# A decoder block on one core: 32 of the 640 dense expert tokens gathered instead, with their buffers, pacing and one inverse root moved

## The chip, the cores and the metric

The kernel runs on one core of a Trainium2 chip. The metric is the device time of one execution in microseconds (us); lower is better. Every time and row below belongs to an execution on the chip.

## The reference

One decoder layer on 1024 tokens of width 1024, in float32:

```python
x = x + concat(gated_deltanet(h), sliding_window_attention(h)) @ w_out
x = x + peer(rmsnorm(x))
x = x + sigmoid(rmsnorm(x) @ w_g) * (p @ w_p)
out = rmsnorm(x)
```

What matters here is `peer`, retrieval of single-neuron experts. For each token and each of 8 heads, two queries are scored against 128 keys each; the best 16 of each half are combined, and of the 256 sums the best 16 name experts out of 128 x 128 = 16384. So each token has 128 experts (8 heads x 16), each with a gate from a softmax over its head:

```python
act = gelu(einsum("td,thkd->thk", x, u_tab[expert]))
y   = einsum("thk,thkd->td", gates * act, v_tab[expert])
```

`u_tab` and `v_tab` have 16384 rows of 1024 float32 each (64 MB a table).

## The kernel before

Tokens are worked in eight blocks of 128. There are three large stages.

**Upstream** (`upstream`, L327). Projections, DeltaNet and attention (`mixing`), then retrieval (`retrieving`, L383) in four groups of two blocks. For a group, `retrieve` (L398) multiplies by the output weights, takes the norm, stores its transposed halves (`h2Td`, L435 and L436, for the dense blocks) or the tokens themselves (`h2d`, L431, for the gathered ones), makes the queries, and takes the top 16 of each half (`first_topk`, L749) and of the combinations (`topk`, L757). `topk` turns positions back into indices with comparisons and sums over 16-wide axes, on a tile of KC = 16 results at a time (L786 to L808). Weights are loaded on SP's queue, four pairs deep.

**Two ways through the experts.** Blocks 0 to 4 (`DBLK`) go the dense way: for them every expert is computed, and a table G of gates, mostly zero, selects. `gbuild` (L837) makes that table for one block in eight slices of 16 tokens (`TB`): for four tokens at a time it compares an iota with the two indices (one VectorE instruction, L845), scales by the gate (four on ScalarE, L847), multiplies (four on TensorE) and copies out; a slice is written to DRAM (`gd`, L853). Blocks 5 to 7 (`ABLK`) go the gathered way: for each of a token's 128 experts one indirect DMA fetches 128 rows of 4 KB, one per token and partition.

**Dense stage** (`dense`, L924). A loop over 128 chunks of 128 experts, in 32 groups of four (`GC`). A chunk loads its 512 KB of each table, splits them into a high and a low part (`split`, L167: ScalarE copies, VectorE subtracts), and multiplies with the 640 dense tokens in two parts of 320 columns, three products (`mm3`, L141) for each of eight slices of the width: 48 matmuls. ScalarE takes the gelu, VectorE multiplies by the group's part of G (`Gt`, loaded at L969), and the product is split again (`wh`, `wl`). After four chunks, each token block is multiplied with the second table in two halves of 512 columns, 30 matmuls a chunk; the tokens are the stationary operand there. Blocks 0 and 1 stay in PSUM to the end (`HELD`), the others are added to `xB` on VectorE (L1009).

**Gathering beside it.** `gather_job` (L904) is a generator that yields after each gather. For a block, `gather_dots` (L862) loads the tokens (`h2n`), fetches 128 times from `u` with a dot product on VectorE each (L868), and takes gelu times gate; `gather_block` (L875) fetches 128 times from `v` with a multiply-add each (L882) into `acc`, which starts as the residual and is stored back. `h2n` and `acc` share one buffer (tag `hacc`). Fetches are issued by POOL (`fetched`, L856). Their tiles alternate between two pools, `gp` with four and `gx` with three buffers, opened after upstream (L1069, L1070), where retrieval's tiles lie before.

What sets the order: the program is scheduled when it is built, by a simulated clock and the order in which it is written, and each engine then runs its own instructions in that fixed order. `step` (L946) hands out gathers evenly over 448 steps (128 chunks and 32 x 10 half blocks):

```python
n = total * count[0] // steps - count[1]
count[1] += n
advance(n)
```

`held_back` (L895) forbids that the VectorE instruction of a gather be placed before the step that lies two (`LAG`) back. DMAs other than gathers go through SP's queue in order.

**Final stage** (`final`, L1013). The last gate for blocks 5, 6, 0, 1, 2, 3, 4, 7 in this order. `pre` (L1033) takes a norm: square with a sum on ScalarE, inverse root on POOL (`rsqrt`, L154: a multiply-add and a power), scaling on VectorE, eight transposes and a split. `gate_weights` (L1020) loads and splits eight 512 KB slices; `post` (L1047) has 48 matmuls of 512 columns a block.

## Time and profile before

| | |
|---|---|
| median of 3 runs | 3034.56 us (3032.35 to 3036.15) |
| the profiled execution | 3043.6 us |
| its span, first to last instruction | 3041.8 us |
| mean granted TensorE clock | 0.986 of 2.4 GHz |
| HBM | 766.40 MB read, 99.61 MB written |
| gathers | 768 (384 from `u`, 384 from `v`) |

In all views PE is TensorE's matmul, PEld its weight load, DVE VectorE, ACT ScalarE, POOL GpSimd and SP SyncE, whose rows are DMA issues. Times are us from the span's start unless marked ns. Busy time of PE is modelled and pipelined: a row's duration is longer than the distance to the next start, so the rate of matmuls is read from starts. A row of groups has the operation, its tiles (out<-in), shapes and count, then busy us and mean ns of one, then the idle time just before them on that engine and what ended most of it. "L79", "L82", "L76" and "L136" are helpers that many places use, so tiles name the operation.

### The profile page before, as it was taken

The numbers are of one execution on the slowest core, as the hardware profiler recorded it, in microseconds if no ns is written. First come the engines' busy times: TensorE is split into PE (matmuls) and PEld (weight loads), VectorE is DVE, ScalarE is ACT, GpSimd is POOL, SyncE is SP. The second block draws the span as 40 slices with busy tenths as digits, with TensorE's granted clock in tenths as the row PEclk, the third lists the DMA queues.
The fourth block names the chain that finished last, engine by engine and source line by source line (L and its number), as shares of the span: only waits on it lengthen the run. The fifth ranks groups of instructions, "written<-read, shape, count | busy, mean of one in ns | idle before, by whom it ended". The sixth has DMA issues, their size and how long they took to land. (4 is left out here: it accounts for less than half of the span.)

```text
span 3041.8 us, 49726 instructions
## 1 busy us (share of the span) xinstructions
PE 2936.2 (97%) x18287; PEld 2690.0 (88%) x18287; DVE 2499.4 (82%) x5023; ACT 1234.6 (41%) x2761; POOL 1068.4 (35%) x901
## 2 busy tenths in 40 slices
PE   7999999999999889999999999999999999999988
PEld 5887999999998789999999989998898898998967
DVE  5658636898999779988699889887998898899974
ACT  5556634488777663222222222232232232222223
POOL 0000000000000000765356556554656565556541
PEclk9989999999999999999999999999999999999989
DMA  7569657689889994999799989888999899899962
GB/s 236 142 223 364 206 191 248 215 223 243 237 242 270 287 279 141 351 338 348 272 342 354 330 319 369 329 332 300 335 351 345 318 358 332 306 337 347 324 256 89
DMA packets 449955, 869.30 MB, mean 286 GB/s; under 512 B 193456, under 2 KB 235824, under 8 KB 445360
## 3 DMA queue, kind: packets, MB, share of 16 engines
q1 hardware_dynamic: 339120, 463.43, 46.5%
q0 software_dynamic: 110592, 402.70, 36.4%
q8 instruction: 143, 2.34, 0.3%
q14 instruction: 100, 0.82, 0.1%
HBM read 766.40 MB, written 99.61 MB: 285 GB/s over the span
## 5 line engine op out<-in xcount | busy, mean ns | idle before, releaser
L136 PE MATMUL bk_u<-hT,uh 128*128 128x320 f32 x4096 | 915.4, 310 | 7.0 <-DMA hT<-h2Td 3.7
L136 PEld LDWEIGHTS bk_u<-hT,uh 128*128 128x128 f32 x4096 | 695.7, 189 | 23.2 <-ACT ge L988 4.6
L858 POOL DMA_INDIRECT rows<-in_u_dram,eidx x384 | 499.1, 1300 | 555.5 <-DVE dots L868 283.1
L136 PE MATMUL bk_u<-hT,ul 128*128 128x320 f32 x2048 | 635.0, 310 | 0.3 <-DVE ul L79 0.3
L858 POOL DMA_INDIRECT rows<-in_v_dram,eidx x384 | 498.6, 1298 | 350.1 <-DVE acc L82 287.5
L82 DVE SCALAR_TENSOR_TENSOR acc<-rows,dots,acc 128x1024 f32<-128x1024 f32 x384 | 492.2, 1282 | 35.4 <-DMA rows<-in_v_dram,eidx 24.5
L868 DVE CUSTOM_DVE_ANT_0 rows<-rows,h2n 128x1024 f32<-128x1024 f32 x384 | 459.9, 1223 | 27.5 <-DMA rows<-in_u_dram,eidx 27.3
L136 PEld LDWEIGHTS bk_u<-hT,ul 128*128 128x128 f32 x2048 | 386.5, 189 | 4.1 <-DVE ul L79 0.7
L988 ACT ACTIVATE ge<-bk_u 128x320 f32<-128x320 f32 x256 | 109.8, 431 | 603.3 <-PE bk_u L136 552.6
L136 PE MATMUL bk_y<-vh,wh 128*128 128x512 f32 x768 | 298.9, 391 | 3.0 <-DVE xB L79 3.0
L136 PE MATMUL bk_y<-vl,wh 128*128 128x512 f32 x768 | 299.9, 392 | 0.0
L136 PE MATMUL bk_y<-vh,wl 128*128 128x512 f32 x768 | 296.8, 393 | 2.6 <-DVE wl L79 2.6
L76 ACT ACTIVATE wh<-ge 128x320 fp32r<-128x320 f32 x256 | 118.7, 469 | 316.7 <-DVE ge L79 304.1
L76 ACT ACTIVATE o<-o,tT 128x128 f32<-128x128 f32 x640 | 204.5, 392 | 56.4 <-DVE o L79 55.1
L76 ACT ACTIVATE uh<-ur 128x1024 fp32r<-128x1024 f32 x128 | 135.3, 1057 | 226.4 <-PE bk_u L136 217.5
L136 PE MATMUL bk_gm<-o 128*128 128x128 f32 x1280 | 203.2, 286 | 22.5 <-ACT o L76 16.2
L136 PE MATMUL bk_s<-h,whi 128*128 128x256 f32 x1024 | 209.1, 295 | 3.3 <-DMA whi<-wqc 1.0
L79 DVE TENSOR_TENSOR o<-iota,tT 128x1024 f32<-128x1024 f32 x160 | 194.7, 1220 | 11.5 <-PE bk_gm L136 8.9
L136 PEld LDWEIGHTS bk_gm<-o 128*128 128x128 f32 x1280 | 178.2, 195 | 29.0 <-ACT o L76 20.2
L136 PE MATMUL bk_yp<-vl,wh 128*128 128x512 f32 x512 | 199.7, 391 | 0.0
L136 PE MATMUL bk_yp<-vh,wh 128*128 128x512 f32 x512 | 199.1, 391 | 0.0
L79 DVE TENSOR_TENSOR xB<-bk_y,xB 128x512 f32<-128x512 f32 x192 | 131.1, 689 | 79.5 <-PE bk_y L136 79.1
(302 smaller groups left out, 5840.5 us busy)
## 6 DMA issues: line engine op xcount, KB each, us to landing
ur<-in_uT_dram SPq DMA_DIRECT2D x128, 512.0 KB, 6.8
vr<-in_v_dram SPq DMA_DIRECT2D x128, 512.0 KB, 6.7
gd<-stage SPq DMA_DIRECT2D x40, 1024.0 KB, 7.3
Gt<-gd SPq DMA_DIRECT2D x32, 1280.0 KB, 9.6
wlo<-wqc SPq DMA_DIRECT2D x128, 256.0 KB, 4.6
whi<-wqc SPq DMA_DIRECT2D x128, 256.0 KB, 4.7
whi<-woc SPq DMA_DIRECT2D x64, 256.0 KB, 4.8
wlo<-woc SPq DMA_DIRECT2D x64, 256.0 KB, 4.7
```

The source lines that it names most:

```text
L76: return S.activation(o, i, AF.Copy, **k)
L79: return V.tensor_tensor(o, a, b, op)
L82: return V.scalar_tensor_tensor(o, a, s, b, op0, op1, **k)
L136: PE.matmul(o, l, r, start=start, stop=stop)
L858: G.indirect_dma_start(out=r, out_offset=None, in_=tab, in_offset=bass.IndirectOffsetOnAxis(ap=eidx[:, u, s:s + 1], axis=0))
L868: held_back(V.tensor_tensor_reduce(out=r, in0=r, in1=h2n, op0=ALU.mult, op1=ALU.add, scale=1.0, scalar=0.0, accum_out=dots[:, s:s + 1]))
L988: S.activation(ge, pa, AF.Gelu_apprx_tanh)
```

## The change

- The last 32 tokens of block 4 leave the dense way. `NU` and `NT` become 608, the parts 304 columns; `gbuild` makes six slices for block 4, and `h2Td`, the second product and the sum into `xB` take 96 tokens of it.
- For these 32 tokens a new `gather_part` runs ahead of block 5. Four slots share a row of partitions: partition 32 g + t holds slots 32 g to 32 g + 31 of token t, so that 32 gathers of 128 rows from each table do for 32 x 128 experts. The indices and gates get into that layout through DRAM (`peidx`, `pegate`), the tokens are stored once (`ph2d`) and loaded four times, and a matmul with a 0/1 matrix (`fold`) adds the four partial sums into the rows of `xB`.
- The pool `gp` is opened before retrieval and has three buffers, `gx` four. To make room, `topk` works on KC = 8 results at a time.
- 832 gathers are handed out over 31/32 of the 448 steps, that is by step 434.
- The first inverse root of the final stage is taken by Newton steps on VectorE.

```diff
+CUT = 32
+NU = len(DBLK) * 128 - CUT
-GBUF = 4
-GXBUF = 3
+GBUF = 3
+GXBUF = 4
+    fold = cp.tile([P, P], F32, name="fold")
+        nc.sync.dma_start(fold, I["fold"])
     def rsqrt(pool, dst, src, scale, n):
+        if newton[0]:
+            v, i, t = (pool.tile([P, n], d, tag=f"rn{m}{n}", name="rn_" + m)
+                       for m, d in (("v", F32), ("i", I32), ("t", F32)))
+            V.tensor_scalar(v, src, scale, EPS, op0=ALU.mult, op1=ALU.add)
+            V.tensor_scalar(i, v.bitcast(I32), 1, None, op0=ALU.logical_shift_right)
+            V.tensor_scalar(i, i, -1.0, 1597463007.0, op0=ALU.mult, op1=ALU.add)
+            y = i.bitcast(F32)
+            for it in range(3):
+                tt(t, y, y, ALU.mult)
+                stt(t, t, -0.5, v, ALU.mult, ALU.mult)
+                stt(dst if it == 2 else y, t, 1.5, y, ALU.add, ALU.mult)
+            return
+            pools["gp"] = ctx.enter_context(tc.tile_pool(name="gp", bufs=GBUF, side="right", reuse_waits="tile"))
             with ExitStack() as es:
                 lt = es.enter_context(tc.tile_pool(name="lt", bufs=1, side="right", reuse_waits="tile"))
+                if b == LB:
+                    nc.sync.dma_start(ph2d, h[LP:P, :])
-        KC = 16
+        KC = 8
+        if b == LB:
+            pe = tk.tile([P, P], I32, tag="pe", name="pe")
+            stt(pe, i1, 128.0, i2, ALU.mult, ALU.add)
+            nc.sync.dma_start(peidx, pe[LP:P, :])
+            nc.sync.dma_start(pegate, ga[LP:P, :])
+            for g in range(P // CUT):
+                nc.sync.dma_start(pidx[g * CUT:(g + 1) * CUT, :], peidx[:, g * CUT:(g + 1) * CUT])
+                nc.sync.dma_start(pgate[g * CUT:(g + 1) * CUT, :], pegate[:, g * CUT:(g + 1) * CUT])
-        for tb in range(P // TB):
+        for tb in range((LP if b == LB else P) // TB):
+    def gather_part():
+        gp = pools["gp"]
+        h2n = gp.tile([P, D], F32, tag="hacc", name="h2n", bufs=1)
+        for g in range(P // CUT):
+            nc.sync.dma_start(h2n[g * CUT:(g + 1) * CUT, :], ph2d)
+        dots = gp.tile([P, P], F32, tag="dots", name="dots", bufs=1)[:, 0:CUT]
+        for s in range(CUT):
+            r = fetched(gp, I["u"], None, s)
+            held_back(V.tensor_tensor_reduce(out=r, in0=r, in1=h2n, op0=ALU.mult, op1=ALU.add, scale=1.0,
+                                             scalar=0.0, accum_out=dots[:, s:s + 1]))
+            yield
+        S.activation(dots, dots, AF.Gelu_apprx_tanh)
+        tt(dots, dots, pgate, ALU.mult)
+        acc = gp.tile([P, D], F32, tag="hacc", name="acc", bufs=1)
+        for s in range(CUT):
+            v = fetched(gp, I["v"], None, s)
+            if s == 0:
+                held_back(V.tensor_scalar(acc, v, dots[:, 0:1], None, op0=ALU.mult))
+            else:
+                held_back(stt(acc, v, dots[:, s:s + 1], acc, ALU.mult, ALU.add))
+            yield
+        xB = pools["xB"]
+        for j in range(2):
+            cs = slice(j * 512, (j + 1) * 512)
+            py = bank("y")
+            mm(py, fold, acc[:, cs])
+            tt(xB[:, len(DBLK) - 1, cs], py, xB[:, len(DBLK) - 1, cs], ALU.add)
+
     def gather_job():
+        yield from gather_part()
         for b in ABLK:
             yield from gather_block(pools["gp"], b)
-            total = len(ABLK) * 2 * P
+            total = len(ABLK) * 2 * P + 2 * CUT
-                n = total * count[0] // steps - count[1]
+                n = min(total, total * count[0] // (steps * 31 // 32)) - count[1]
-                            ts_ = slice(bi * P, (bi + 1) * P)
-                            mm3(py, wh[:, ts_], wl[:, ts_], vh[:, cs], vl[:, cs],
+                            ts_ = slice(bi * P, min((bi + 1) * P, NT))
+                            mm3(py[0:ts_.stop - ts_.start], wh[:, ts_], wl[:, ts_], vh[:, cs], vl[:, cs],
-                            last = tt(xB[:, bi, cs], py, xB[:, bi, cs], ALU.add)
+                            np_ = min(P, NT - bi * P)
+                            last = tt(xB[0:np_, bi, cs], py[0:np_], xB[0:np_, bi, cs], ALU.add)
+            newton[0] = True
             nxt = pre(order[0])
+            newton[0] = False
-    pools["gp"] = ctx.enter_context(tc.tile_pool(name="gp", bufs=GBUF, side="right", reuse_waits="tile"))
```

## Rows read from the trace of the kernel before

**Rows 1.** The page, part 1: busy time, share, instructions of two engines.

```profile
PE 2936.2 (97%) x18287; PEld 2690.0 (88%) x18287; DVE 2499.4 (82%) x5023; ACT 1234.6 (41%) x2761; POOL 1068.4 (35%) x901
```

**Rows 2.** Windows by stage: us, PE, PEld, DVE, ACT, POOL busy, PEclk, DMA share, GB/s.

```profile
600.00:1000.00 400.00, 381.77 (x3160) 369.46 (x3159) 377.43 (x1249) 310.04 (x925) 19.45 (x29) 0.99 0.89 244
1000.00:1125.00 125.00, 109.34 (x813) 105.67 (x812) 100.90 (x335) 83.56 (x230) 0.75 (x2) 0.92 0.96 275
1125.00:2920.00 1795.00, 1783.52 (x9960) 1621.35 (x9958) 1574.46 (x2372) 478.27 (x778) 992.42 (x765) 1.00 0.89 326
1225.00:1450.00 225.00, 225.00 (x1267) 205.28 (x1267) 201.27 (x335) 59.29 (x96) 148.36 (x109) 1.00 0.94 347
1775.00:1825.00 50.00, 45.74 (x239) 40.20 (x238) 37.67 (x52) 9.84 (x15) 28.50 (x21) 0.96 0.86 303
...
2920.00:2935.00 15.00, 2.56 (x11) 1.96 (x10) 11.87 (x11) 2.90 (x4) 6.11 (x6) 0.63 0.75 286
...
1250.00:1300.00 50.00, 50.00 (x285) 45.78 (x285) 44.22 (x77) 12.55 (x22) 34.20 (x25) 1.00 1.00 385
```

**Rows 3.** Timeline of PE, three starts: second product, first product, second product again.

```profile
2299.75 0.39 PE L136 MATMUL bk_y<-vl,wh 128*128 128x512 f32 x1
...
2302.95 0.31 PE L136 MATMUL bk_u<-hT,ul 128*128 128x320 f32 x1
...
2304.56 0.39 PE L136 MATMUL bk_y<-vh,wh 128*128 128x512 f32 x1
```

**Rows 4.** Groups of instructions, whole span: the table's builder, then `topk`.

```profile
L76 ACT ACTIVATE o<-o,tT 128x128 f32<-128x128 f32 x640 | 204.5, 392 | 56.4 <-DVE o L79 55.1
...
L79 DVE TENSOR_TENSOR o<-iota,tT 128x1024 f32<-128x1024 f32 x160 | 194.7, 1220 | 11.5 <-PE bk_gm L136 8.9 <-ACT tT L76 1.6 <-ACT o L76 0.7
...
L79 DVE TENSOR_TENSOR get<-get 128x1024 bf16<-128x1024 bf16 x24 | 16.5, 689 | 0.2
...
L79 DVE TENSOR_TENSOR get<-pos,sel_b 128x2048 bf16<-128x2048 bf16 x8 | 9.8, 1225 | 0.0
```

**Rows 5.** Timeline where gathering begins: VectorE in block 7's `topk`, then POOL.

```profile
1187.44 0.66 DVE L773 MAX8 bs<-cand 128x8 f32<-128x50 f32 x5
...
1220.28 0.94 POOL L858 DMA_INDIRECT rows<-in_u_dram,eidx  x1 [47.07 <-DVE cand L79]
```

**Rows 6.** Groups of VectorE's instructions from 1224 to 2900 us.

```profile
L82 DVE SCALAR_TENSOR_TENSOR acc<-rows,dots,acc 128x1024 f32<-128x1024 f32 x365 | 467.9, 1282 | 30.4 <-DMA rows<-in_v_dram,eidx 19.8 <-DMA acc<-x1d 7.5
L868 DVE CUSTOM_DVE_ANT_0 rows<-rows,h2n 128x1024 f32<-128x1024 f32 x383 | 458.7, 1223 | 27.5 <-DMA rows<-in_u_dram,eidx 27.3
L79 DVE TENSOR_TENSOR vl<-vr,vh 128x1024 fp32r<-128x1024 f32 x119 | 145.4, 1222 | 17.4 <-ACT vh L76 17.2
L79 DVE TENSOR_TENSOR ul<-ur,uh 128x1024 fp32r<-128x1024 f32 x118 | 144.3, 1223 | 20.5 <-ACT uh L76 20.5
L79 DVE TENSOR_TENSOR xB<-bk_y,xB 128x512 f32<-128x512 f32 x179 | 122.0, 688 | 77.3 <-PE bk_y L136 77.1
L79 DVE TENSOR_TENSOR ge<-ge,Gt 128x320 f32<-128x320 f32 x240 | 116.7, 490 | 25.1 <-ACT ge L988 24.8
L79 DVE TENSOR_TENSOR wl<-ge,wh 128x320 fp32r<-128x320 f32 x240 | 116.4, 489 | 7.3 <-ACT wh L76 7.1
```

**Rows 7.** Timeline around the dense stage's end: ScalarE, POOL, TensorE and VectorE.

```profile
2913.97 0.18 ACT L190 ACTIVATION_READ_ACCUMULATOR h<-xt 128x1 f32 x1
2926.17 1.06 ACT L76 ACTIVATE wgh<-raw 128x1024 fp32r<-128x1024 f32 x1 [12.02 <-DMA raw<-in_wg_dram]
...
2926.81 0.19 POOL L156 TENSOR_SCALAR rs_v<-ss 128x1 f32<-128x1 f32 x1
...
2932.81 1.97 PE L139 MATMUL bk_tp<-ident,h 128*128 128x128 f32 x8 [12.44 <-DVE h L82]
...
2938.53 1.28 DVE L82 SCALAR_TENSOR_TENSOR acc<-rows,dots,acc 128x1024 f32<-128x1024 f32 x1
```

More of the change, by code (lines that the diff above doesn't have):

```diff
@@ L33 @@
 BBLK = HBLK + DBLK
-NU = len(DBLK) * 128
+CUT = 32
+NU = len(DBLK) * 128 - CUT
 GC = 4
 TB = 16
-GBUF = 4
-GXBUF = 3
+GBUF = 3
+GXBUF = 4
 RATE = 0.6
@@ L71, in block_kernel @@
     NB = len(BBLK)
-    NT = NB * P
+    NT = NB * P - CUT
+    LB = DBLK[-1]
+    LP = P - CUT
     NH = len(HBLK) * P
@@ L149, in block_kernel @@
     gd = dr.tile([NE // GC, P, NT // TB, GC, TB], F32, name="gd")
+    pidx = cp.tile([P, CUT], I32, name="pidx")
+    pgate = cp.tile([P, CUT], F32, name="pgate")
+    peidx = dr.tile([CUT, P], I32, name="peidx")
+    pegate = dr.tile([CUT, P], F32, name="pegate")
+    ph2d = dr.tile([CUT, D], F32, name="ph2d")
+    newton = [False]
     eidx = cp.tile([P, len(UBLK), P], I32, name="eidx")
@@ L432, in retrieve @@
                 transpose_split("s3", h, h2h, h2l, bs_)
+                if b == LB:
+                    nc.sync.dma_start(ph2d, h[LP:P, :])
                 if b in DBLK:
                     t0 = (b - DBLK[0]) * P
-                    nc.sync.dma_start(h2Td[0][:, :, t0:t0 + P], h2h.bitcast(F32)[:, :, bs_])
-                    nc.sync.dma_start(h2Td[1][:, :, t0:t0 + P], h2l.bitcast(F32)[:, :, bs_])
+                    n = LP if b == LB else P
+                    ns = slice(bi * P, bi * P + n)
+                    nc.sync.dma_start(h2Td[0][:, :, t0:t0 + n], h2h.bitcast(F32)[:, :, ns])
+                    nc.sync.dma_start(h2Td[1][:, :, t0:t0 + n], h2l.bitcast(F32)[:, :, ns])
             tv = [lt.tile([P, 16, 16], F32, tag="tv", name="tv", bufs=2) for _ in grp]
@@ L858, in fetched @@
         G.indirect_dma_start(out=r, out_offset=None, in_=tab,
-                             in_offset=bass.IndirectOffsetOnAxis(ap=eidx[:, u, s:s + 1], axis=0))
+                             in_offset=bass.IndirectOffsetOnAxis(
+                                 ap=pidx[:, s:s + 1] if u is None else eidx[:, u, s:s + 1], axis=0))
         return r
@@ L940, in dense @@
             parts = [(n0, min(width, NU - n0)) for n0 in range(0, NU, width)]
-            total = len(ABLK) * 2 * P
+            total = len(ABLK) * 2 * P + 2 * CUT
+            pools["xB"] = xB
             steps = NE + NE // GC * NB * 2
@@ L1088, in _host @@
         "consts": _consts(),
+        "fold": ((np.arange(P)[None, :] >= P - CUT)
+                 & (np.arange(P)[:, None] % CUT == np.arange(P)[None, :] % CUT)).astype(np.float32),
         "x": a["x"][0],
```

## The prediction

> **What bounds the kernel now.** I read the busy time by engine first [rows 1], then the stretches [rows 2]. TensorE is busy for 97% of the span and VectorE for 82%, but the stages differ. The stretch to look at is the dense one, 1125 to 2920 us: TensorE 1783.5 of 1795 us at a granted clock of 1.00, that is 2.4 GHz, so 11.5 us are lost in all of it. VectorE has 1574 of 1795, the DMA engines a share of 0.89. The stretch is bound by TensorE, with two others close behind. The spacing of its matmuls stands in the timeline [rows 3]: from the first start to the second lie 14 matmuls of 512 columns (3.20 us, 228.6 ns each), from the second to the third 11 of 320 columns (1.61 us, 146.4 ns). Check: a chunk of 128 experts has 48 of the latter and 30 of the former, 7.03 + 6.86 = 13.89 us, times 128 is 1777 us.
>
> The profiled execution took 3043.6 us (span 3041.8); the median of the runs shown is 3034.56. I sum against 3043.6 and carry the 9.0 us between them to the end.
>
> **The change part by part.**
>
> *Fewer columns.* 608 dense tokens instead of 640 make the first product 304 columns wide. From the two spacings a column costs (228.6 - 146.4)/192 = 0.428 ns and a matmul 9.4 ns beside its columns; 16 columns are 6.85 ns, over 128 x 48 = 6144 matmuls **-42 us**. The second product has its tokens in the stationary operand: 96 of them in the last block cost as much as 128, so nothing is gained there. A chunk then takes 13.56 us. All of this lies on the path as long as TensorE is the bound.
>
> *A shorter table for the last dense block.* Six of eight slices are built. Left out are 8 VectorE comparisons at 1.22 us, 32 ScalarE scalings at 0.39 us (12.5 us) [rows 4], 32 matmuls and 2 DMA writes. They sit in 1000 to 1125 us, where TensorE is busy 109 of 125 us and DMA at 0.96 [rows 2], and the first dense gate multiply waits for the load of what they write. Between 0 and -12.5; I take **-6**, since other work (group 3's queries) shares the stretch.
>
> *Top-k in two halves.* 18 instructions per block become 36 of half the size; half of 2048 elements costs 689 and not 612 ns [rows 4], so 2 x 689 - 1225 = 153 ns more each, 2.8 us a block. Five blocks run ahead of the dense stretch: 13.8 us at most, 0 if covered. VectorE is busy 377 of 400 us there [rows 2], so the cover is thin: **+5**. The other three fall on the start of the dense stretch, under TensorE.
>
> *Indices, token copies, fold.* One 128 x 128 multiply-add on VectorE, two writes and eight small reads through DRAM on SP's queue. The reads wait for the writes to land, and group 3's weight loads stand behind them in that queue: 0 to 5 us. Four small loads of the tokens. On TensorE two unsplit matmuls of 512 columns, 0.23 to 0.9 us each, which wait for the last multiply-add of the part. Then block 5 may load its tokens into the buffer that the fold read, and SP waits for it with expert loads queued behind. The nearest row is the hand-over from block 5 to block 6, which has the same single buffer: TensorE 45.7 of 50 us [rows 2], 4.3 lost. Bounds 1 to 12, **+6** in all.
>
> *64 more gathers, in less time.* Beside TensorE now; the question is whether they stay there. Before, the rows alternate between two pools, and gathering starts only once block 7's retrieval has freed its tiles, at 1220 us [rows 5]. Opening one pool early frees only the even rows; the odd ones still wait behind it in POOL's order. I take a start at 1205, between 1188 (block 7's candidates made [rows 5]) and 1222. By TensorE alone the dense part ends at 1125 + 128 x 13.56 + 11.5 = 2872. The counter hands out all 832 gathers by step 434 of 448, one group (54 us) earlier, 2818. That leaves 1613 us: 0.516 gathers per us. The best long stretch before is 109 in 225 us, 0.484 per us, TensorE 225.0 of 225 [rows 2].
>
> VectorE's need: its rows give 1.25 us a gather, and 2 x 1.22 + 4 x 0.49 + 1.5 x 0.69 = 5.4 us a chunk [rows 6]. For 1225 to 1450 that is 109 x 1.25 + 16.2 x 5.4 = 224 against 201.3 shown, so starts overlap by a tenth: 1.125 and 4.9 us, 4.8 with the narrower chunk. After: 832 x 1.125 + 119 x 4.8 = 1507. Waits for rows, 27.3 + 19.8 = 47.1 us [rows 6], grow with the count to 51. A change between dot products and sums costs 7 us of gathering (37.7 busy of 50, where 0.895 x 50 = 44.7 would be usual [rows 2]); there are 7 of these instead of 5: 49. Sum 1607 of 1613, and some 18 us may trail behind the dense end, as the last gathered sum does before, at 2938 [rows 7]. So 24 us are spare, and VectorE's other waits (77.1 + 24.8 + 20.5 + 17.2 + 7.1 = 147 us [rows 6]) must nearly vanish. Most come from VectorE being ahead of TensorE and would go when it is late. If all went the cost is 0, if all stayed 123. I let 42 us stay, nearer the low end for that reason: 42 - 24 = **+18**.
>
> *The end.* Before, the square sum of block 5 is ready at 2914, but its root stands behind the last gathers in POOL's queue, at 2926.8, and TensorE sits idle 12.4 us until 2932.8; the stretch 2920 to 2935 has TensorE 2.6 us busy at a clock of 0.63 [rows 2, 7]. On VectorE the root is 12 small instructions; five maxima take 0.66 us there [rows 5], so some 1.6 us, ahead of the dense end. What is late next is the first gate weight: its load waits for the last dense matmuls, and ScalarE splits it at 2926.2 to 2927.2 [rows 7]. So about 2933 + 1.8 of transposes becomes 2927.2: -7.4, and a shorter spell at half clock. Between 0 and -15; **-9**.
>
> Sum: -42 - 6 + 5 + 6 - 9 = -46 without crowding, -28 with it: 3015.6, less 9.0 is **3006.6 us**.
>
> **The rivals.**
>
> *A, slower: VectorE takes TensorE's place in the dense part.* For it: 1607 of 1613 us are filled, and VectorE runs in order, so a late row holds up the gate multiplies behind it. Against it: at 0.484 gathers per us TensorE lost nothing. It decides once 70 of the 147 us stay (70 - 24 = 46, the whole gain). With 88, three in five: 3043.6 - 46 + 64 - 9.0 = 3052.6. Chance 0.15.
>
> *B: the DMA engines cannot carry it.* A chunk moves 1.36 MB (two loads of 512 KB, a quarter of the table) in 13.56 us, 100 GB/s; 832 gathers of 512 KB are 436 MB. The turn is at the rate with which the gathers end 18 + 46 us past 2818: 436 MB in 2882 - 1205 - 49 = 1628 us, 268 + 100 = 368 GB/s. For it: 347 GB/s already take a share of 0.94. Against it: 385 over 50 us at a share of 1.00 [rows 2]. At a ceiling of 365: 436/265 = 1646, the end at 2900, 64 us past 2836; 3052.6 as well. Chance 0.07. The page DMA: Bandwidth & Descriptors of the Trainium skill (Where 436 GB/s comes from) has some 358 GB/s per core for loads from HBM; by that rule 436/258 = 1690, 108 us late, an estimate of 3097. The 385 over 50 us differ from it, and the measurement decides.
>
> *C: no crowding.* VectorE's waits vanish with its slack: -46, 2988.6. Chance 0.20.
>
> *D: the change does not do what it says*, the narrower matmul taking as long as before: -28 + 42, 3048.6. The spacings of two widths [rows 3] speak against it. Chance 0.03.
>
> **How the numbers follow.** The forecast keeps 0.55. It and C are faster: 0.75. B near the turn and the upper side of the forecast make 0.08 within 0.2%, which is 6 us and about what a measurement of this kernel can tell from no change; the rest of A, B and D is slower, 0.17. The range reaches from 2984 (C, and a little more at the end) to 3044: it takes in the forecast with its bounds and the near half of A, and leaves out the far half of A and B. For the forecast alone it would be 2994 to 3024.
>
> **What would show it.** Matmuls of the first product every 139.6 ns; 832 gathers, the first near 1205 and the last landing before the dense end; VectorE at 0.93 or more between 1225 and 2820, with its wait for xB well under 77 us; TensorE's loss in the dense part some 25 to 35 us instead of 11.5; no idle of 12 us at its end, and the first root there not on POOL. Wrong would be: waits of TensorE for VectorE of 50 us and more; DMA shares at 1.00 through the stretch; or a dense part that begins over 10 us later, the halved top-k being dearer than taken.

## The result, and the profile after

The kernel after takes 3180.82 us (median of 4 runs, 3175.59 to 3189.22) where the kernel before took 3035.36 beside it: a ratio of 1.048 (95% interval 1.046 to 1.051), 145 us slower. 3006.6 was predicted, faster, so it is 174 us off and on the other side. The profiled execution of after has a span of 3187.4 us, 145.6 more than before's 3041.8.

**Where the 145.6 us lie.** The gate multiply of the first product (`ge`) marks the ends of the dense part. The view of one tile's instructions gives count, shortest/median/longest ns, and first and last start, here of after and then of before:

```profile
L82 DVE TENSOR_TENSOR ge<-ge,Gt x256: 451/466/548, 1120.5 to 2978.6; 128x304 f32<-128x304 f32 x128
```

```profile
L79 DVE TENSOR_TENSOR ge<-ge,Gt x256: 474/489/556, 1132.9 to 2895.3; 128x320 f32<-128x320 f32 x128
```

Up to the first one after is 12.4 us ahead; between first and last it takes 1858.1 us against 1762.4, 95.7 more, though the narrower product alone was to take 42 off; from the last to the end of the span 208.8 against 146.5, 62.3 more. -12.4 + 95.7 + 62.3 = 145.6. In the text below "dense part" and "end" are these two distances.

The narrower product itself does what was expected of it. In the timeline of TensorE 15 matmuls lie between these two starts, 2.09 us, 139.3 ns each (139.6 was predicted, 146.4 stood in [rows 3]):

```profile
1895.45 0.30 PE L141 MATMUL bk_u<-hT,ul 128*128 128x304 f32 x1
...
1897.54 0.30 PE L141 MATMUL bk_u<-hT,ul 128*128 128x304 f32 x1
```

Two windows of after, the first to be held against [rows 2]: us, PE, PEld, DVE, ACT and POOL busy, PEclk, DMA share, GB/s.

```profile
1125.00:2920.00 1795.00, 1697.32 (x9550) 1499.08 (x9549) 1507.60 (x2364) 456.66 (x749) 1209.14 (x732) 0.98 0.85 311
...
1100.00:1450.00 350.00, 280.00 (x1589) 246.81 (x1589) 284.31 (x705) 80.28 (x132) 176.65 (x109) 0.91 0.74 261
```

From 1125 to 2920 TensorE loses 97.7 us where it lost 11.5, most of it early: from 1100 to 1450 it is busy 280.0 of 350 us, where the same window of before shows

```profile
1100.00:1450.00 350.00, 345.30 (x1974) 316.40 (x1973) 306.75 (x737) 110.49 (x191) 156.19 (x116) 0.99 0.83 296
```

The granted clock fell with these waits, to 0.91 of 2.4 GHz in that window (0.99 in before), so some of the 280.0 us ran at 1.2 GHz; over the whole span it is 0.967 where before has 0.986.

But VectorE has not become the bound, as rival A had it: it is busy 1507.6 us, less than the 1574 of before. Nor have the DMA engines: a share of 0.85 instead of 0.89. The engine that has more is POOL, 1209 instead of 992 us with fewer instructions. The costliest groups of after (busy us, mean ns | idle before):

```profile
L894 POOL DMA_INDIRECT rows<-in_u_dram,eidx x384 | 627.7, 1635 | 283.3 <-DVE dots L905 190.5
L894 POOL DMA_INDIRECT rows<-in_v_dram,eidx x384 | 629.3, 1639 | 237.8 <-DVE acc L85 138.0
...
L85 DVE SCALAR_TENSOR_TENSOR acc<-rows,dots,acc 128x1024 f32<-128x1024 f32 x415 | 531.0, 1279 | 105.0 <-DMA rows<-in_v_dram,eidx 89.1
L905 DVE CUSTOM_DVE_ANT_0 rows<-rows,h2n 128x1024 f32<-128x1024 f32 x384 | 460.0, 1217 | 100.5 <-DMA rows<-in_u_dram,eidx 96.6
...
L141 PE MATMUL bk_y<-vh,wh 128*128 128x512 f32 (+1 forms) x768 | 309.8, 405 | 65.8 <-DVE xB L82 65.8
```

VectorE waits 186 us for rows over the whole span (52 in before, 47 of them in the window of [rows 6]), and TensorE 65.8 us for sums into `xB`. Three things are behind it, and each is seen in one place.

**One gather per group is held for 3 to 19 us.** Timelines of VectorE and of POOL around such a place (start, us, engine, line, operation):

```profile
1699.98 0.68 DVE L82 TENSOR_TENSOR xB<-bk_y,xB 96x512 f32<-96x512 f32 x1
...
1704.11 0.68 DVE L82 TENSOR_TENSOR xB<-bk_y,xB 96x512 f32<-96x512 f32 x1
...
1715.97 0.46 DVE L82 TENSOR_TENSOR wl<-ge,wh 128x304 fp32r<-128x304 f32 x1
1716.35 0.46 DVE L82 TENSOR_TENSOR ge<-ge,Gt 128x304 f32<-128x304 f32 x1
1723.56 1.28 DVE L85 SCALAR_TENSOR_TENSOR acc<-rows,dots,acc 128x1024 f32<-128x1024 f32 x1 [6.75 <-DMA rows<-in_v_dram,eidx]
```

```profile
1699.99 0.94 POOL L894 DMA_INDIRECT rows<-in_v_dram,eidx  x1 [0.30 <-issue]
1701.23 16.39 POOL L894 DMA_INDIRECT rows<-in_v_dram,eidx  x1 [0.30 <-issue]
1717.93 0.94 POOL L894 DMA_INDIRECT rows<-in_v_dram,eidx  x1 [0.30 <-issue]
```

The median gather instruction takes POOL 1.0 to 1.2 us. The one at 1701.23 takes 16.39. VectorE meanwhile runs on without a gap until 1716.81; then the rows are used up, it waits 6.75 us, and the held gather ends 0.8 us into that wait. As it looks here, VectorE starves itself: while it runs on, POOL does not get to ask for the rows that VectorE will need. There are 31 of over 3 us in after, 333 us together. In before none of the 768 takes more than 2.63.

**The start.** TensorE waits for a sum into `xB` that VectorE takes up only behind the last top-k (`eidx` at 1221.35); timelines of TensorE and VectorE:

```profile
1222.29 0.80 PE L141 MATMUL bk_y<-vh,wh 128*128 128x512 f32 x1 [34.64 <-DVE xB L82]
```

```profile
1221.35 0.29 DVE L85 SCALAR_TENSOR_TENSOR eidx<-cand 128x128 int32<-128x128 f32 x1
1221.55 1.28 DVE L82 TENSOR_TENSOR xB<-bk_y,xB 128x512 f32<-128x512 f32 x2
```

**The end.** 61 sums of gathered rows stand in VectorE's order behind the last dense sum (3008.57), where before has 8. Block 7's final is last and needs them: TensorE waits 39 us for its `h`. One row of the view by tile, one of the timeline:

```profile
L85 DVE SCALAR_TENSOR_TENSOR acc<-rows,dots,acc x61: 1271/1278/1317, 3009.2 to 3149.6; 128x1024 f32<-128x1024 f32 x61
```

```profile
3160.30 1.94 PE L144 MATMUL bk_tp<-ident,h 128*128 128x128 f32 x8 [39.24 <-DVE h L85]
```

### The profile page after: what moved, and what is told of

It is laid out like the page before. It is cut to its first block, busy times and chain, and to the rows that moved or that the text cites. A ratio compares the mean times of both kernels' runs of the same rounds, so it can differ in the third digit from the quotient of the medians.

```text
span 3187.4 us, 50006 instructions
## 1 busy us (share of the span) xinstructions
PE 2926.8 (92%) x18227; PEld 2628.9 (82%) x18227; DVE 2575.2 (81%) x5271; ACT 1214.6 (38%) x2722; POOL 1438.7 (45%) x963
## 4 chain that ended last, share of the span: by engine, by line
PE 33%; issue 30%; DMA 13%; POOL 10%; DVE 10%; ACT 2%; SPq 0%; POOLq 0%; DVEq 0%; ACTq 0%
POOL rows L894 10%; PE bk_acc L141 7%; PE bk_u L141 6%; PE bk_y L141 5%; DMA rows<-in_v_dram,eidx 4%; PE bk_s L141 4%; DMA rows<-in_u_dram,eidx 4%; PE bk_yp L141 2%; PE bk_g L141 2%; PE bk_dn L141 2%; DVE acc L85 2%; DVE rows L905 1%; PE bk_gm L141 1%; DVE get L82 1%; PE bk_sw L141 1%
## 5 line engine op out<-in xcount | busy, mean ns | idle before, releaser
L141 PE MATMUL bk_u<-hT,uh 128*128 128x304 f32 x4096 | 873.7, 304 | 10.1 <-ACT ge L1055 5.1
L894 POOL DMA_INDIRECT rows<-in_u_dram,eidx x384 | 627.7, 1635 | 283.3 <-DVE dots L905 190.5
L894 POOL DMA_INDIRECT rows<-in_v_dram,eidx x384 | 629.3, 1639 | 237.8 <-DVE acc L85 138.0
L141 PE MATMUL bk_u<-hT,ul 128*128 128x304 f32 x2048 | 618.2, 302 | 0.5 <-DVE ul L82 0.5
L141 PE MATMUL bk_y<-vh,wh 128*128 128x512 f32 (+1 forms) x768 | 309.8, 405 | 65.8 <-DVE xB L82 65.8
L79 ACT ACTIVATE wh<-ge 128x304 fp32r<-128x304 f32 x256 | 115.0, 456 | 559.3 <-DVE ge L82 461.1
L141 PE MATMUL bk_y<-vh,wl 128*128 128x512 f32 (+1 forms) x768 | 303.9, 401 | 2.8 <-DVE wl L82 2.7
L141 PE MATMUL bk_y<-vl,wh 128*128 128x512 f32 (+1 forms) x768 | 305.7, 400 | 0.0
L141 PEld LDWEIGHTS bk_y<-vh,wh 128*128 128x128 f32 (+1 forms) x768 | 140.4, 183 | 107.5 <-DVE xB L82 71.5
L141 PE MATMUL bk_yp<-vh,wl 128*128 128x512 f32 x512 | 185.4, 402 | 14.9 <-DVE wl L82 14.7
```

Source lines behind the costliest of these rows:

```text
L79: return S.activation(o, i, AF.Copy, **k)
L141: PE.matmul(o, l, r, start=start, stop=stop)
L894: G.indirect_dma_start(out=r, out_offset=None, in_=tab, in_offset=bass.IndirectOffsetOnAxis(ap=pidx[:, s:s + 1] if u is None else eidx[:, ...
```

## The experiments

All times are medians, each ratio is against the kernel before on the same chip (3034.7 to 3036.3 us there).

| run | us | ratio (95%) | longest gather, us | dense part | end |
|---|---|---|---|---|---|
| after | 3180.8 | 1.046 to 1.051 | 19.3 | 1858 | 209 |
| low_two_input | 3177.3 | 1.044 to 1.048 | 14.7 | 1864 | 201 |
| low_one_input | 3133.5 | 1.028 to 1.035 | 8.1 | 1804 | 208 |
| before_plus_two | 3092.5 | 1.016 to 1.020 | 3.6 | 1803 | 161 |
| before_plus_one | 3094.7 | 1.018 to 1.022 | 7.2 | 1785 | 159 |
| before_96 | 3097.3 | 1.018 to 1.028 | 16.5 | 1809 | 148 |
| before_96_32 | 3051.0 | 1.004 to 1.007 | 3.6 | 1770 | 153 |
| full_rows | 3122.0 | 1.026 to 1.029 | 3.2 | 1801 | 205 |
| late_pool | 3189.2 | 1.049 to 1.053 | 13.7 | 1844 | 206 |
| full_rows_late | 3146.7 | 1.034 to 1.037 | 3.2 | 1815 | 202 |
| part_second | 3151.7 | 1.035 to 1.041 | 3.2 | 1842 | 178 |
| part_second_pin | 3153.5 | 1.036 to 1.042 | 3.6 | 1881 | 143 |
| columns_only | 3043.3 | 1.002 to 1.004 | 3.2 | 1734 | 177 |
| columns_pin | 3081.7 | 1.013 to 1.017 | 4.5 | 1806 | 141 |
| columns_light_pin | 3060.6 | 1.007 to 1.010 | 2.3 | 1785 | 141 |
| columns_no_load | 3042.4 | 1.001 to 1.004 | 3.9 | 1759 | 140 |
| full_rows_no_load | 3074.5 | 1.011 to 1.015 | 3.6 | 1812 | 142 |
| before_newton | 3039.4 | 1.000 to 1.003 | 2.5 | 1755 | 154 |
| before_newton_pin | 3051.1 | 1.003 to 1.007 | 3.2 | 1782 | 142 |

Before's profile has 2.6, 1762 and 147 in the last three columns. "Longest gather" is over the whole span. Several of these kernels leave work out to separate causes: in the two `low` runs and in columns_light_pin the low parts of the expert weights are copies, the `columns` runs give the 32 tokens no expert sum, before_96 drops rows 96 to 127 of 64 sums, and the two runs without loads work with the first chunk's weights throughout. The diffs are shortened.

### Is it the two operands, or VectorE's load?

The first theory was that of the timeline: VectorE without a gap, in instructions with two operands in SBUF, keeps POOL out. Theory 2: VectorE is simply too full. Two pairs, each differing in one kind of instruction:

```diff
 low_one_input / low_two_input, after with, in place of split(ur, uh, ul), and so for v:
+copy(uh, ur)
+copy(ul, ur)
+V.tensor_reduce(junk(), uh, AX, ALU.max)          # one
+tt(ur, ur, uh, ALU.subtract)                      # two
 before_plus_one / before_plus_two, before with:
 split(ur, uh, ul)
+V.tensor_reduce(junk(), uh, AX, ALU.max)          # one
+tt(ur, ur, uh, ALU.subtract)                      # two
```

> The kernel after, with the low parts of the expert weights written by ScalarE (a copy of the raw tile, so the second terms of the split products are not the real residuals) and in place of each subtraction on VectorE a maximum over the same 1024 columns: about as long, but one operand read from SBUF instead of two. Theory 1 (POOL's gather instruction is held up for as long as VectorE runs on without a gap through instructions with two operands in SBUF): gather instructions of over 3 us fall from 31 to under 10, and the time falls by 40 us or more, under 3140. Theory 2 (VectorE simply has more work than TensorE's time leaves it): as many long gathers as in the other kernel of this pair, and a time within 20 us of it.

> The partner of the run before: ScalarE writes the low parts too (also a copy of the raw tile, not the real residuals), but VectorE still subtracts two SBUF tiles, into the raw tile that nobody reads any more. VectorE and ScalarE have as many instructions, of about the same length, as in the partner. Theory 1: still 20 or more gathers of over 3 us, time 3150 to 3200. Theory 2: the same time as the partner within 20 us.

> The kernel before with one more VectorE instruction per chunk of 128 experts: a maximum over 1024 columns of one SBUF tile into one column, 128 times some 1.1 us, as much work as VectorE's waits in the dense stretch. Theory 1: VectorE is full but leaves gaps in its second operand's reads; under 10 gathers of over 3 us, time 3035 to 3090. Theory 2: 3060 to 3150, the same as its partner within 20 us.

> The kernel before with one more VectorE instruction per chunk of 128 experts: a subtraction of two SBUF tiles of 1024 columns into a tile that nobody reads any more, 128 times some 1.2 us. Theory 1: 15 or more gathers of over 3 us where the kernel before has none, and 3100 to 3200, at least 30 us above its partner. Theory 2: the same as its partner within 20 us.

The first pair is 44 us apart, with instructions of the same length (1.21 and 1.22 us): gathers of over 3 us take 142 us together with one operand and 273 with two. But they are as many (31 and 33), which theory 1 had otherwise. The pair also differs in what is written, one column or 1024, the latter into the tile that the next load needs. That it is the operand that lets a gather through is seen in where the held ones end in low_one_input: 20 of the 31 within 0.9 us of the start of such a maximum, 10 in a gap of VectorE (in low_two_input 3 of 33 end in the subtraction that stands in its place). One of the 20, at 2602.72:

```profile
2598.36 4.36 POOL L894 DMA_INDIRECT rows<-in_u_dram,eidx  x1 [3.13 <-DVE dots L905]
```

```profile
2602.22 1.21 DVE L1028 TENSOR_REDUCE jk<-uh 128x1 f32<-128x1024 f32 x1
```

The second pair speaks against both theories as the cause. With VectorE busy 0.92 of the time from 1450 to 2850 (0.87 in before) and with two operands, before gets 57 us slower, but only six gathers take over 3 us, none over 3.6 (the one of 7.2 in its partner lies at 1152, amid the top-k), and the pair is 2 us apart. In before itself, worked out from the starts in its timeline, VectorE runs 50 us on end without a gap from 2418, and the 25 gathers in that time take 1.9 us at most. A full VectorE costs time, but something in after must be there for a gather to be held.

The page SBUF — State Buffer of the Trainium skill (Who interferes with whom) says that a VectorE instruction with two SBUF inputs and a GpSimd instruction that reads SBUF exclude each other, the later one waiting for the other to finish. The gather reads its indices from SBUF. The first pair agrees with it, and so do gathers of up to 2.6 us in before, a VectorE instruction or two; a hold of 16 us across a dozen of them is more than that.

### The sums over 96 rows

Each of the 31 held gathers of after starts within 9 us of a VectorE instruction over 96 partitions: the sums of the last dense block, two per group, seen at 1699.98 above. Theory 3: those are the trigger. It was put into the kernel before alone, and taken out of after alone.

```diff
 before_96:
-last = tt(xB[:, bi, cs], py, xB[:, bi, cs], ALU.add)
+np_ = 96 if bi == NB - 1 else P
+last = tt(xB[0:np_, bi, cs], py[0:np_], xB[0:np_, bi, cs], ALU.add)
 before_96_32, behind it:
+if np_ < P:
+    last = tt(xB[np_:P, bi, cs], py[np_:P], xB[np_:P, bi, cs], ALU.add)
 full_rows, after with wh and wl of NB * P columns, and
+copy(wh[:, NT:], zcol)
+copy(wl[:, NT:], zcol)
-ts_ = slice(bi * P, min((bi + 1) * P, NT))
+ts_ = slice(bi * P, (bi + 1) * P)
-last = tt(xB[0:np_, bi, cs], py[0:np_], xB[0:np_, bi, cs], ALU.add)
+last = tt(xB[:, bi, cs], py, xB[:, bi, cs], ALU.add)
```

> The kernel before, with the two sums per group of the last dense block taken over 96 of its 128 rows (rows 96 to 127 of that block's products are left out); nothing else differs, and VectorE's order is that of before. Theory 3 (the VectorE instruction over 96 partitions is what upsets POOL: from it on, until VectorE has its first gap, a gather instruction that meets a row of VectorE instructions does not get through): one long gather per group, 20 or more over 3 us where before has none, and 3060 to 3150. Theory 1 (VectorE's two-operand instructions alone) and theory 2 (VectorE full): no gather over 3 us, 3030 to 3040, for VectorE has no more work than before.

> The kernel after, with the second product of the last dense block kept at 128 rows: its stationary operand gets 32 columns of zeros, written by ScalarE, and the sum into xB runs over all 128 partitions. Theory 3: fewer than 5 gathers of over 3 us instead of 31; the loss of TensorE from 1450 to 2900 us falls from some 90 to under 35 us, the time to 3040 to 3100 (the losses at the start of the dense part, some 55 us more than before, and the sums that the order has behind the dense part stay). Theories 1 and 2: 25 or more long gathers still, 3165 to 3200.

> The kernel before, with each sum of the last dense block in two instructions, over rows 0 to 95 and right behind it over rows 96 to 127; all is computed. If the uneven load of the partitions' quarters is the trigger (the quarter left out runs ahead until VectorE's next gap): the second instruction evens it only where it follows directly, so clearly fewer long gathers than the 30 of the run with 96 rows alone, under 12, and under 3075. If any instruction over part of the partitions is the trigger: 25 or more long gathers, 3085 to 3130.

The gathers from 1225 to 2900 us by table (count: shortest/median/longest ns), in before, in before_96, in before_96_32 and in full_rows:

```profile
L858 POOL DMA_INDIRECT rows<-in_u_dram,eidx x377: 932/1242/1992, 1224.9 to 2657.4; - x189
L858 POOL DMA_INDIRECT rows<-in_v_dram,eidx x371: 932/1017/2625, 1449.0 to 2898.9; - x186
```

```profile
L858 POOL DMA_INDIRECT rows<-in_u_dram,eidx x377: 932/1240/13722, 1226.8 to 2688.1; - x189
L858 POOL DMA_INDIRECT rows<-in_v_dram,eidx x352: 932/1020/15959, 1461.7 to 2899.6; - x176
```

```profile
L858 POOL DMA_INDIRECT rows<-in_u_dram,eidx x378: 932/1242/3618, 1224.8 to 2673.3; - x189
L858 POOL DMA_INDIRECT rows<-in_v_dram,eidx x362: 932/1136/3217, 1449.0 to 2899.1; - x181
```

```profile
L896 POOL DMA_INDIRECT rows<-in_u_dram,eidx x384: 932/1227/1992, 1324.8 to 2798.3; - x192
L896 POOL DMA_INDIRECT rows<-in_v_dram,eidx x307: 932/1019/3198, 1577.6 to 2898.8; - x154
```

The medians lie within 0.12 us of each other; what differs is the longest, and with it how many are done by 2900. Before with 64 of its sums a quarter smaller, no other change and the same order on VectorE, has 30 held gathers, 297 us together, and is 61 us slower. After with full rows has two, of 3.2 us, and is 59 us faster than after. The windows from 1450 to 2850 of after and of full_rows:

```profile
1450.00:2850.00 1400.00, 1372.81 (x7740) 1215.27 (x7739) 1182.03 (x1679) 364.32 (x598) 985.02 (x595) 0.99 0.88 323
```

```profile
1450.00:2850.00 1400.00, 1397.36 (x7949) 1255.61 (x7948) 1211.19 (x1702) 398.04 (x822) 790.46 (x606) 1.00 0.89 329
```

TensorE loses 2.6 us there instead of 27 and gets 209 more matmuls done. Theory 3 is shown in both directions, for this one shape: 96 of 128 rows, one operand from PSUM and one from SBUF. And the run with a second sum over the other 32 rows (directly behind the first in 62 of 64 places) has no more than two of over 3 us either: the partitions left out are what matters, not the smaller instruction. Why a gather is then held, no run shows; that the quarter left out runs ahead until VectorE's next gap, as the expectation had it, was argued only. The 16 us that before_96_32 costs go with its 64 instructions more (some 44 us of VectorE); no run separates them.

### The start: when the first gathers come

With full rows 3122 us are left, 87 above before. Theory 4 looks for them at the start.

```diff
 late_pool, after with; full_rows_late: full_rows with; part_second: full_rows_late with the second edit:
-pools["gp"] = ...            (ahead of retrieval)
+pools["gp"] = ...            (behind upstream(), as in before)
 def gather_job():
-    yield from gather_part()
-    for b in ABLK:
+    yield from gather_block(pools["gp"], ABLK[0])
+    yield from gather_part()
+    for b in ABLK[1:]:
 part_second_pin and the other pins, in step(), sums being the list of held_back instructions:
+done = len(sums) - 16
+if done > 0:
+    tc.add_manual_dep(ins.ins, sums[done].name, ...)      # order only
```

> The kernel after, with the first pool of row buffers opened behind retrieval as in the kernel before, all else as in after. If the early gathers cost the start of the dense part (VectorE's sums of products wait behind them, TensorE 34.6 us for one sum): TensorE busy 310 or more of the 350 us from 1100 to 1450 instead of 280, and 20 to 45 us less time than after. If the 64 more gathers or the order cost it however late they start: within 10 us of after, and TensorE still under 290.

> Both edits together: full 128 rows in the last dense block's sums, and the first pool of row buffers opened behind retrieval. If the two losses are separate: the savings of the two runs add up within 15 us. If the stalls are all that matters: as the run with full rows alone, within 10 us.

> As the run with full rows and the late pool, but the 32 tokens are gathered behind block 5 instead of ahead of it. Theory 4 (the start of the dense part loses 55 to 80 us because the first gathers stand at the front: their sums wait on VectorE behind the last top-k, and TensorE's fold, in program order after few groups, waits for them): TensorE busy 335 or more of the 350 us from 1100 to 1450, no wait of over 10 us for a sum, time 3050 to 3090. Rival (64 more gathers cost the same wherever they stand): TensorE under 310 there or as much lost around the fold later, time over 3110.

> The same, with VectorE's order pinned: each dense step's last VectorE instruction comes behind the sums handed out up to 16 gathers earlier, so that none of the 832 stands behind the dense part (45 do without it, 61 in after). Theory 5 (the planner that writes the order takes VectorE for full and defers sums which the chip has time for): the dense part is at most 15 us longer than without the pin, and the time 20 to 50 us less. Rival (VectorE has no time for them): the dense part longer by what the end saves, time within 12 us of the run without it, or more.

None of the four comes out as its first theory had it. Opening the pool late is no gain: late_pool takes 8 us more than after, full_rows_late 25 more than full_rows. The 34.6 us for `xB` are gone in both, so they came with the early pool, but TensorE waits 55 us for the part's sum at the fold, which stands in its fixed order. With the part second TensorE has 341 of 350 us up to 1450, as theory 4 wanted, and then loses 95 us in one place. TensorE's timeline of full_rows_late, and its waits in part_second:

```profile
1352.82 3.78 PE L143 MATMUL bk_y<-acc,fold 128*128 128x512 f32 x4 [55.17 <-DVE acc L85]
```

```profile
PE bk_y L143 <- DVE acc L85: 95.0, 1, 95.0
```

So the fold is a barrier: wherever it stands, TensorE stops there until VectorE has caught up with the gathers, and the lateness that would otherwise be carried to the end is paid at once. The pin moves 45 trailing sums into the dense part: the end goes from 178 to 143 us, the dense part from 1842 to 1881, and the time stays. So this order gains nothing; VectorE is busy 0.875 of the time from 1450 to 2850 in it, so that it is simply full is not shown.

### The columns without the gathers

```diff
 columns_only, full_rows_late with:
-yield from gather_part()
-total = len(ABLK) * 2 * P + 2 * CUT
+total = len(ABLK) * 2 * P
 columns_light_pin, with the pin and, in place of both splits:
+copy(uh, ur)
+copy(ul, ur)
 columns_no_load, full_rows_no_load: ur and vr loaded once ahead of the loop over chunks
```

> After with full rows and the late pool, and without the 64 gathers of the 32 tokens, their products and the fold (the 32 tokens get no expert sum): what is left of the change is the narrower product, the shorter table, the halved top-k, the pace of 31/32 and the first root. If these terms are as predicted (-42 - 6 + 5 - 9, some -50): 2980 to 3000. If the gathers' rate is what bounds the dense part now, so that narrower products bring little: 3015 to 3045, with 40 or more sums behind the last dense sum.

> As the run of the columns alone (the 32 tokens get no expert sum), with the order pinned so that no sum of gathered rows stands behind the dense part (46 did). If only the planner's order held the sums back: the dense part still ends near 2890 and the time is 2985 to 3015. If the chip cannot bring or take 768 rows in the shorter dense part: TensorE waits in it for VectorE, 30 us or more in all, and the time stays over 3025.

> The same, and in addition ScalarE writes the low parts of the expert weights (a copy of the raw tile, so not the real residuals) and VectorE has no instruction for them, 256 of 1.2 us less. Theory 6 (VectorE's time is what the sums lack): TensorE's waits fall under 20 us and the time is 2975 to 3005, 20 us or more below the run with the pin alone. Theory 7 (the DMA engines, at some 330 GB/s, are what the rows lack): the same time as the run with the pin alone within 10 us, with VectorE waiting for rows 60 us or more.

> As the run of the columns alone (no gathers for the 32 tokens, which get no expert sum), without a pin, and without the loads of the dense part's expert weights: the first chunk's tiles are loaded once and split again for every chunk, so all 128 chunks compute with chunk 0's weights. All engines have the same instructions; the DMA engines have 1 MB per chunk less of about 4.3. The order that the planner then writes has no sum behind the dense part (46 did). Theory 7 (what the rows lack is DMA, in the planner's reckoning and on the chip): rows at 0.457 per us or more, the pace asked for, instead of 0.435, and 2975 to 3000 us. If it is VectorE: the same rate as before, 3025 or more.

> As the run with full rows (all 832 gathers, first pool opened early), without the loads of the expert weights in the same way (all chunks compute with chunk 0's weights). Theory 7 in full: the 64 gathers are nearly free once there is DMA for them, 2985 to 3030, within 40 us of the run without them, what is left being the start's wait for the top-k on VectorE. If the gathers of the 32 tokens cost by their place at the start, whatever the DMA engines have to do: 70 us or more above the run without them.

The columns and the rest of the change without the gathers bring nothing: 1.003 (1.002 to 1.004). The gate multiplies and the trailing sums of columns_only say where the gain went:

```profile
L82 DVE TENSOR_TENSOR ge<-ge,Gt x256: 450/466/545, 1127.9 to 2862.1; 128x304 f32<-128x304 f32 x128
```

```profile
L85 DVE SCALAR_TENSOR_TENSOR acc<-rows,dots,acc x46: 1270/1277/1324, 2888.7 to 3005.0; 128x1024 f32<-128x1024 f32 x46
```

The dense part is 28.2 us shorter than in before, the end 30.2 us longer. 768 gathers used to fit beside 1762 us of TensorE; beside 1734, in the order written, they do not, 46 sums come behind, and block 7's final waits for them. The windows from 1450 to 2850 of columns_only, columns_light_pin, columns_no_load and full_rows_no_load, in that order:

```profile
1450.00:2850.00 1400.00, 1393.15 (x7932) 1252.87 (x7932) 1214.75 (x1665) 399.51 (x820) 777.77 (x608) 1.00 0.89 329
```

```profile
1450.00:2850.00 1400.00, 1379.87 (x7797) 1237.18 (x7797) 1004.86 (x1444) 568.70 (x1014) 749.96 (x617) 0.99 0.89 332
```

```profile
1450.00:2850.00 1400.00, 1386.98 (x7879) 1246.41 (x7878) 1247.72 (x1659) 390.07 (x811) 857.14 (x630) 1.00 0.77 262
```

```profile
1450.00:2850.00 1400.00, 1383.67 (x7845) 1240.77 (x7844) 1283.71 (x1751) 389.79 (x814) 915.59 (x674) 1.00 0.80 278
```

POOL's count is here the count of gathers: 608 in 1400 us, 0.434 per us. VectorE with 210 us less to do (theory 6) gets 0.441 where columns_pin has 0.438, and the kernel takes 3060.6, 21 us less than columns_pin and still 17 more than columns_only; theory 6 falls as the explanation of the rate. With a quarter fewer bytes for the DMA engines (theory 7) full_rows reaches 0.481, no sum trails, and the time falls from 3122.0 to 3074.5. Do the rows come sooner then? VectorE's waits from 1450 to 2850 (total us, times, longest) in full_rows and in full_rows_no_load:

```profile
DVE xB L82 <- PE bk_y L143: 90.7, 65, 6.1
DVE rows L907 <- DMA rows<-in_u_dram,eidx: 27.0, 23, 5.3
...
DVE acc L85 <- DMA rows<-in_v_dram,eidx: 8.9, 8, 2.1
```

```profile
DVE rows L907 <- DMA rows<-in_u_dram,eidx: 30.8, 33, 3.8
...
DVE xB L82 <- PE bk_y L143: 22.9, 33, 2.3
...
DVE acc L85 <- DMA rows<-in_v_dram,eidx: 6.8, 7, 1.6
```

VectorE waits as long for rows without the loads as with them, 38 and 36 us. What falls is its wait for TensorE's products, from 91 to 23 us. So with the loads in place VectorE is ahead of TensorE through this stretch and stands idle for it, while sums of gathered rows are kept for the end. In the order that is written without the loads they stand earlier, and none trails. The gain is seen in the order; that the DMA engines themselves kept rows back is not shown by this pair. Nor is it ruled out: columns_pin, which has the loads and no trailing sum, waits 59 us for rows in this stretch where columns_only waits 33, and is 38 us slower. And theory 7 falls short as a promise: columns_no_load stays at 3042.4. Its end is 37 us shorter than that of columns_only, but its dense part begins 13 us later and is 25 us longer: the order now has more sums early, and TensorE has 318 of the 350 us up to 1450 instead of 341. How much of the limit is the order and how much the chip stays open.

### The root on VectorE

```diff
 before_newton, before with:
+newton[0] = True
 nxt = pre(order[0])
+newton[0] = False
 before_newton_pin, the same with the pin
```

> The kernel before with the first inverse root of the end on VectorE and nothing else. Predicted term: -9, between 0 and -15, so 3021 to 3036; no idle of 12 us of TensorE ahead of the first transpose of the end. Rival (the next wait, for the last gathers' sums or the gate weights, takes its place): within 3 us of before.

> The kernel before with the first inverse root on VectorE and the order pinned, so that 3 sums of gathered rows instead of 8 stand behind the last dense sum, and the root's instructions stand ahead of few of them. If the root was worth nothing only because of the sums around it: 3018 to 3030, TensorE's wait for the first h under 12 us instead of 21. If the late rows themselves set it: within 4 us of before.

The root alone gains nothing, 1.0015 (1.0001 to 1.0029); with the pin it is slower. Timelines of ScalarE, VectorE and TensorE in before_newton:

```profile
2903.21 0.18 ACT L204 ACTIVATION_READ_ACCUMULATOR h<-xt 128x1 f32 x1
```

```profile
2917.38 2.60 DVE L82 SCALAR_TENSOR_TENSOR acc<-rows,dots,acc 128x1024 f32<-128x1024 f32 x2 [2.81 <-DMA rows<-in_v_dram,eidx]
2919.90 0.15 DVE L160 TENSOR_SCALAR rn_v<-ss 128x1 f32<-128x1 f32 x1
...
2927.31 0.15 DVE L82 SCALAR_TENSOR_TENSOR rs<-rn_t,rn_i 128x1 f32<-128x1 f32 x1
```

```profile
2929.91 3.68 PE L139 MATMUL bk_tp<-ident,h 128*128 128x128 f32 x16 [21.00 <-DVE h L82]
```

The square sum is there at 2903.4, the chain begins at 2919.9, behind sums that wait for their rows, and takes 7.6 us because sums and gate weights stand between its 12 instructions. POOL's queue has been exchanged for VectorE's, and the same late rows stand ahead in both. In before this was already to be seen: the root is done on POOL at 2927.7, and VectorE takes up `h` only behind two more such sums:

```profile
2928.95 2.60 DVE L82 SCALAR_TENSOR_TENSOR acc<-rows,dots,acc 128x1024 f32<-128x1024 f32 x2 [3.02 <-DMA rows<-in_v_dram,eidx]
2931.48 1.28 DVE L82 SCALAR_TENSOR_TENSOR h<-xt,rs,ple_norm 128x1024 f32<-128x1024 f32 x1
```

No version that was run is faster than the kernel before.

## Why the prediction was wrong

By medians the 145.5 us divide as 59 (after less full_rows), 79 (full_rows less columns_only: the 64 gathers, their fold, the early pool) and 8 (columns_only less before: the rest of the change). By the prediction's sum they were to be 0, 24 (6 for the fold and its hand-over, 18 of crowding) and -52 (-42 - 6 + 5 - 9). The three errors of 59, 55 and 60 us make up the 174. The middle one is no fixed price of 64 gathers: without the loads they cost 32 us (3074.5 less 3042.4).

1. **The step that failed first: "96 of them in the last block cost as much as 128, so nothing is gained there".** It was looked at for TensorE's time alone, and there it holds: worked out from the starts in after's timeline, matmuls on 96 tokens follow each other every 0.232 us, those on 128 every 0.233. But the smaller sum on VectorE holds up one of POOL's gathers per group, and without it the kernel is 59 us faster. No row of before could price it, since no VectorE instruction of its dense part covers fewer than 128 partitions; but that it was a new shape in the loop was there in the diff, and it got no bounds.
2. **The crowding of VectorE, +18.** Its rate was held against the best stretch, 109 gathers in 225 us (0.484 per us, [rows 2]), and 0.516 was asked for. By 2818, when all 832 were to be issued, after has issued 698 and full_rows 714; from 1450 to 2850 no kernel that loads its expert weights got over 0.455. (The 0.44 of before there, 616 gathers, is no limit: its counter asks for no more, 768 in 1762 us.) The step that failed is that VectorE's other waits would nearly vanish, 42 us of 147 staying, and that the counter's step 434 is the time at which gathers are done. In full_rows, where no gather is held for long, these waits are 153 us from 1224 to 2900 and those for rows 54 (51 had been reckoned): VectorE went on waiting for TensorE, and 62 sums stand behind the dense part, 61 in after, where the prediction had "some 18 us". In after it waits 69 us in that way and 183 for rows. A stretch in which one engine is served best is no proof that the rate can be held. The early pool brought the first gather to 1028 instead of 1205, but only 14 were issued by 1205, and it cost TensorE the 34.6 us for `xB`.
3. **The columns, -42.** A matmul every 139.3 ns, as predicted, and a dense part 28 us shorter where it is alone. The size of the term is right, its place on the path is not: gathers were as close to the bound as TensorE, and the end took back 30 us. The prediction let TensorE's saving count in full as long as TensorE was the bound, but a span that ends with block 7 is bound by the later of the two.
4. **Fold and hand-over, +6.** A wait of 6.7 us for the part's sum in after is near it by luck, because TensorE had lost 34.6 us for `xB` shortly before. With the pool late it is 55 us, with the part second 95.
5. **The end, -9.** It was taken that the root would run ahead of the dense end, in 1.6 us. In before_newton it runs at 2919.9 to 2927.5, and TensorE waits 21 us for `h`.
6. **Table, top-k, indices, -6 + 5 and part of +6.** The first gate multiply is 5 us earlier in columns_only, 12 in after: in its bounds.

Rival A came nearest, with TensorE waiting for VectorE for over 50 us, which was named as a wrong sign. Of its mechanism one half came, late rows that hold up what stands behind them in VectorE's order; the other did not, since VectorE was less busy than before. Its price of 46 us over the forecast was about a quarter of what came. Rival B's ceiling was not met (shares of 0.85 to 0.9 in the dense part), though the time falls when the loads are taken away, as the last pair shows.

## What to carry to other kernels

When a change makes one instruction of a loop cover fewer partitions than its neighbours, look at what the other engine does from there on, and not only at the instruction's own time; padding the operand to 128 rows was worth 59 us here. Where POOL issues gathers and VectorE consumes them, read the longest gather and not only the median: the medians of the four kernels above lay within 0.12 us of each other, the longest at 2.6, 16.0, 3.6 and 3.2 us. Then ask which of the two waits: where VectorE waits longer for TensorE than for rows, it is the order of its instructions that keeps the sums back. And where two engines end close together, a saving on the one is worth only what the other has to spare: a rate is to be taken from the whole stretch, and what is behind the last wait is to be followed to the end of the span.

## What the runs showed of the hardware

- A VectorE sum over partitions 0 to 95, among instructions over all 128, is followed by gathers on POOL that are held for up to 16.5 us in before_96 and 19.3 in after. 24 of the 31 in after, all of over 8 us among them, and 23 of the 30 in before_96 end 0.4 to 0.8 us after the start of VectorE's next gap, however short (0.12 us at 1879.0 sufficed); two of over 8 us in before_96 end without a gap. With a sum over partitions 96 to 127 directly behind (before_96_32), or over all 128 (full_rows), no gather is held over 3.6 us. In the other kernels without a 96-row sum the longest is 4.5, but for one of 7.2 amid the top-k of before_plus_one.
- One operand in SBUF instead of two, in 256 of VectorE's instructions, went with shorter holds (the longest 8.1 instead of 14.7 us) and 44 us less time; 20 of 31 holds then ended within 0.9 us of the start of such an instruction.
- Gathers ran at 0.42 to 0.46 per us from 1450 to 2850 in every kernel that loads its expert weights, with VectorE 72 to 92% busy; without these loads at 0.45 and 0.48.
- The 96 of 128 columns of the stationary operand gave TensorE nothing: a matmul of 512 columns every 0.232 us in after, against 0.233 with 128.
